# Row softmax on one core: stores moved from the load queue to a queue of their own, with a ring of three large slots

## The chip, the cores and the metric

The kernel runs on one core of a Trainium2 chip. The metric is device time in microseconds (us), the median of several executions. Ratios between kernels are the mean time of one kernel's fast runs over the mean time of the other's fast runs of the same rounds, so they are not quite the ratio of the medians quoted beside them.

## The reference

```python
def setup_inputs():
    batch, seq, dim = 32, 512, 1024
    return {"x": np.random.randn(batch, seq, dim).astype(np.float32), "temperature": 0.5}

def reference(x, temperature):
    scaled = x / temperature
    shifted = scaled - np.max(scaled, axis=-1, keepdims=True)
    exp_x = np.exp(shifted)
    return (exp_x / np.sum(exp_x, axis=-1, keepdims=True)).astype(np.float32)
```

There are 16,384 rows of 1,024 floats: 67.1 MB are read and 67.1 MB written. With 128 partitions each partition handles 128 rows of 4 KiB.

## The kernel before

All data passes through one ring in SBUF, 48 rows per partition. The kernel loads 8 rows per partition at a time (4 MiB, one contiguous piece of 32 KiB per partition), so the ring has six slots. VectorE takes the maximum of a group of four rows, ScalarE computes the exponentials and their sums in place, VectorE divides in place, and the slot is stored.

```python
LOADS = [8] * 16
STORES = [[8]] * 16
RING = 48
GROUP = 4
AHEAD = 2
# ... (cut)
    with tc.tile_critical():
        for kind, i, after in _queue(LOADS, STORES, places, AHEAD):
            if kind == "load":
                for b in range(after + 1):          # stores that free this slot
                    if b > done_to:
                        nc.sync.wait_ge(stored[b], 16)
                # ... nc.sync.dma_start(ring <- x).then_inc(loaded[i], 16)
            else:
                nc.sync.wait_ge(scaled, part_end[i])
                # ... nc.sync.dma_start(out <- ring).then_inc(stored[i], 16)
        # ...
        for g in range(len(groups)):
            exponential(g)                          # ScalarE's whole program

        for g in range(len(groups) + 1):            # VectorE's program
            if g < len(groups):
                maximum(g); shift(g)                # maximum waits for loaded[i]
            if g > 0:
                invert(g - 1); divide(g - 1)        # divide raises scaled
```

`_queue` puts loads and stores into one fixed order for SP's queue. `AHEAD = 2` means that two more stores are issued before SP waits for the store that frees a slot for the next load.

## Time and profile before

| | before |
|---|---|
| time, median of the first 3 runs | 321.85 us (321.15 to 322.12) |
| span of the profiled run | 319.9 us |
| VectorE (DVE) busy | 235.4 us, 74% |
| ScalarE (ACT) busy | 149.6 us, 47% |
| the one data queue busy | 97.9% of the span of 16 DMA engines |
| moved | 134.22 MB, mean 420 GB/s |

From the page of before, the span in 40 slices (tenths of the 16 DMA engines' time, then GB/s) and the queue table:

```profile
DMA  8999999999999999999999999999999999999992
GB/s 328 406 447 443 410 459 406 386 448 438 418 451 406 447 422 430 443 418 434 434 426 443 426 430 431 430 447 422 430 419 434 438 426 434 434 426 443 430 430 115
...
q1 hardware_dynamic: 4608, 134.22, 97.9%
```

The DMA engines are full in every slice but the first and the last. Single slices scatter because a transfer's bytes count in the slice where a packet is recorded; the mean of the 38 slices between is 430.

The costliest groups of the same page (line, engine, operation, busy us and mean ns, then idle time before it and who ended it):

```profile
L131 ACT ACTIVATE ring<-ring,bias 128x1024 f32<-128x1024 f32 x128 | 145.4, 1137 | 145.9 <-DVE bias L123 145.9
L113 DVE TENSOR_REDUCE top<-ring 128x4 f32<-128x4096 f32 x32 | 141.3, 4416 | 59.7 <-DMA ring<-in_x_dram 59.7
L150 DVE TENSOR_SCALAR ring<-ring,recip 128x1024 f32<-128x1024 f32 x128 | 87.7, 749 | 1.1
```

Both compute engines have slack. VectorE waits 59.7 us for loads; it isn't the bottleneck.

The DMA issues on SP's queue up to 92 us, without the first six loads, from the timeline of before (start us, duration us; the first line merges three issues, and its duration runs from the first to the last of them):

```profile
32.87 29.88 SPq L171 DMA_DIRECT2D out_dram<-ring  x3
72.68 0.34 SPq L165 DMA_DIRECT2D ring<-in_x_dram  x1
77.19 0.33 SPq L171 DMA_DIRECT2D out_dram<-ring  x1
82.36 0.34 SPq L165 DMA_DIRECT2D ring<-in_x_dram  x1
91.97 0.33 SPq L171 DMA_DIRECT2D out_dram<-ring  x1
92.35 0.43 SPq L165 DMA_DIRECT2D ring<-in_x_dram  x1
```

The load at 72.68 waited for the first store. The second and third stores had been issued before it (the x3 of the first line), so the DMA engines had work while the load was being released.

**A bookkeeping for the DMA engines.** The trace holds a record for each packet of data. The records don't name the engine; a packet that starts where another ends, within a few ns, is taken as its successor on the same engine. Undisturbed, a 32 KiB packet takes 1.213 us and the next one on its engine starts 4 ns before it ends, so one engine needs 1.209 us per 32 KiB and 16 engines move 433.6 GB/s. 134.22 MB at that rate are 309.5 us. For any run I split the time until the last transfer's completion arrives, 0.3 to 0.4 us after the last packet ends, into three parts: *work* (309.5 us, always the same), *idle* (engines with no packet, as a mean over the 16) and *slow* (the remainder: packets that took longer than usual). For before, the last completion arrives at 318.4 us: 309.5 work + 6.2 idle + 2.7 slow. The last 1.5 us of the span follow it. Of the 6.2 us idle, 2.2 are the start; most of the rest is the end, where the engines finish 4.8 us apart.

### The profile page before, as it was taken

The page shows a single profiled execution, that of the slowest core. Times are in us where ns is not written, and L with a number is a line of the kernel's source. Part 1 is how long each engine was busy: PE and PEld are TensorE (multiplying, and loading weights), DVE is VectorE, ACT ScalarE, POOL GpSimd, SP SyncE. Part 2 cuts the span into 40 slices and gives each one's busy share as a digit, 9 for nine tenths or more (in the row PEclk, how much of TensorE's full clock was granted, in tenths as well). Part 3 has the DMA queues.
Part 4 walks back from the last instruction along what each step waited for, and adds up shares of the span by engine and source line. Part 5 has one row for each costly group of instructions (what it writes and reads, how often), then busy time and mean ns, then how long its engine had stood idle before and what let it go on. Part 6 is the DMA issues. An engine that isn't in the chain of part 4 may idle for free.

```text
span 319.9 us, 568 instructions
## 1 busy us (share of the span) xinstructions
DVE 235.4 (74%) x224; ACT 149.6 (47%) x257; POOL 0.2 (0%) x4
## 2 busy tenths in 40 slices
DVE  0399999999996966939679495794948949498300
ACT  1076666665555551635516355163553625546000
POOL 0000000000000000000000000000000000000000
DMA  8999999999999999999999999999999999999992
GB/s 328 406 447 443 410 459 406 386 448 438 418 451 406 447 422 430 443 418 434 434 426 443 426 430 431 430 447 422 430 419 434 438 426 434 434 426 443 430 430 115
DMA packets 4612, 134.25 MB, mean 420 GB/s; under 512 B 512, under 2 KB 512, under 8 KB 512
## 3 DMA queue, kind: packets, MB, share of 16 engines
q1 hardware_dynamic: 4608, 134.22, 97.9%
q14 instruction: 4, 0.03, 0.0%
HBM read 67.11 MB, written 67.11 MB: 420 GB/s over the span
## 4 chain that ended last, share of the span: by engine, by line
DMA 60%; DVE 30%; ACT 3%; issue 0%; SPq 0%
DMA ring<-in_x_dram 35%; DMA out_dram<-ring 26%; DVE top L113 18%; DVE ring L150 11%; ACT ring L131 3%; DVE bias L123 1%; DVE recip L144 0%; SPq L219 0%; SPq L156 0%
## 5 line engine op out<-in xcount | busy, mean ns | idle before, releaser
L131 ACT ACTIVATE ring<-ring,bias 128x1024 f32<-128x1024 f32 x128 | 145.4, 1137 | 145.9 <-DVE bias L123 145.9
L113 DVE TENSOR_REDUCE top<-ring 128x4 f32<-128x4096 f32 x32 | 141.3, 4416 | 59.7 <-DMA ring<-in_x_dram 59.7
L150 DVE TENSOR_SCALAR ring<-ring,recip 128x1024 f32<-128x1024 f32 x128 | 87.7, 749 | 1.1
L131 ACT ACTIVATION_READ_ACCUMULATOR ring<-ring,bias 128x1 f32 x128 | 23.9, 187 | 0.0
L144 DVE RECIPROCAL recip<-sums 128x4 f32<-128x4 f32 x32 | 5.5, 171 | 2.0 <-ACT ring L131 2.0
L123 DVE TENSOR_SCALAR bias<-top 128x4 f32<-128x4 f32 x32 | 5.4, 170 | 1.1
L131 ACT ACT_TABLE_LOAD x1 | 1.3, 1283 | 0.9 <-SPq L156 0.9
L205 POOL MEMSET const-bfloat16-1.0<- 128x1 bf16 x1 | 0.1, 101 | 0.0
L205 POOL MEMSET const-uint8-127<- 128x1 uint8 x1 | 0.1, 101 | 0.0
L205 POOL MEMSET const-float32-0.0<- 128x1 f32 x1 | 0.1, 98 | 0.2 <-issue 0.2
L205 POOL MEMSET const-float32-1.0<- 128x1 f32 x1 | 0.1, 98 | 0.0
## 6 DMA issues: line engine op xcount, KB each, us to landing
ring<-in_x_dram SPq DMA_DIRECT2D x16, 4096.0 KB, 49.0
out_dram<-ring SPq DMA_DIRECT2D x16, 4096.0 KB, 40.5
```

The costliest lines, as they stand in the source:

```text
L113: nc.vector.tensor_reduce(out=top[:, r : r + k], in_=ring[:, s : s + k, :], axis=mybir.AxisListType.X, op=extreme,).then_inc(topped, 1)
L123: nc.vector.tensor_scalar_mul(bias[:, r : r + k], in0=top[:, r : r + k], scalar1=-scale).then_inc(biased, 1)
L131: ins = nc.scalar.activation(ring[:, s + a, :], ring[:, s + a, :], mybir.ActivationFunctionType.Exp, bias=bias[:, r + a : r + a + 1], scal ...
L144: nc.vector.reciprocal(recip[:, r : r + k], sums[:, r : r + k]).then_inc(inverted, 1)
L150: ins = nc.vector.tensor_scalar_mul(ring[:, s + a, :], in0=ring[:, s + a, :], scalar1=recip[:, r + a : r + a + 1])
L205: nc = _bacc.Bacc("TRN2", target_bir_lowering=False, num_devices=1)
```

## The change

Loads stay on SP's queue; stores go on ScalarE's. Neither queue has an order relative to the other: a load waits only for the stores that covered its slot, a store only for its division. The ring becomes three slots of 16 rows, so a transfer is 8 MiB in pieces of 64 KiB. The last 32 rows are handled in smaller parts. The intent is larger pieces and no fixed order that could hold back a ready transfer.

```diff
-LOADS = [8] * 16
-STORES = [[8]] * 16
+LOADS = [16] * 7 + [8] * 2
+STORES = [[16]] * 6 + [[8, 8]] + [[8]] * 2
 RING = 48
 GROUP = 4
-AHEAD = 2
 # ... (_queue and the loop over it removed)
+    def load(i):
+        # ... waits on nc.sync for stored[] of the parts that cover this slot
+        nc.sync.dma_start(out=ring[:, s : s + k, :], in_=dram(xf, r, k, i)).then_inc(
+            loaded[i], 16
+        )
+    def store(n):
+        l, s, r, k = parts[n]
+        nc.scalar.wait_ge(scaled, part_end[n])
+        nc.scalar.dma_start(out=dram(of, r, k, l), in_=ring[:, s : s + k, :]).then_inc(
+            stored[n], 16
+        )
 # ...
-        for g in range(len(groups)):
-            exponential(g)
+        for i in range(len(LOADS)):
+            load(i)
+        # ... SP waits for the stores that are left
+        for g in range(len(groups) + 1):
+            if g < len(groups):
+                exponential(g)
+            for n in range(len(parts)):
+                if part_end[n] == g:
+                    store(n)
```

VectorE's program is unchanged. On VectorE, a slot's last group is divided only after the maximum of the next slot's first group, which waits for the next load. In ScalarE's program, the store stands behind the exponentials of that same group.

More of the change, by code (lines that the diff above doesn't have):

```diff
@@ L28, in _places @@
     return places
-def _queue(loads, stores, places, ahead):
-    flat = [(i, n) for i, ks in enumerate(stores) for n in range(len(ks))]
-    last = {i: n for n, (i, _) in enumerate(flat)}
-    order, given = [], 0
-    for i, k in enumerate(loads):
-        over = [
-            b
-            for b in range(i)
-            if places[b] < places[i] + k and places[i] < places[b] + loads[b]
-        ]
-        after = max((last[b] for b in over), default=-1)
-        while given <= after + ahead and after >= 0 and flat[given][0] < i:
-            order.append(("store", given, None))
-            given += 1
-        order.append(("load", i, after))
-    order += [("store", n, None) for n in range(given, len(flat))]
-    return order
 @with_exitstack
@@ L153, in divide @@
         ins.then_inc(scaled, 1)
-    done_to = -1
-    with tc.tile_critical():
-        for kind, i, after in _queue(LOADS, STORES, places, AHEAD):
-            if kind == "load":
-                for b in range(after + 1):
-                    if b > done_to:
-                        nc.sync.wait_ge(stored[b], 16)
-                done_to = max(done_to, after)
-                s, r, k = places[i], first[i], LOADS[i]
-                nc.sync.dma_start(
-                    out=ring[:, s : s + k, :], in_=dram(xf, r, k, i)
-                ).then_inc(loaded[i], 16)
-            else:
-                l, s, r, k = parts[i]
-                nc.sync.wait_ge(scaled, part_end[i])
-                nc.sync.dma_start(
-                    out=dram(of, r, k, l), in_=ring[:, s : s + k, :]
-                ).then_inc(stored[i], 16)
-        for b in range(len(parts)):
-            if b > done_to:
-                nc.sync.wait_ge(stored[b], 16)
-        for g in range(len(groups)):
-            exponential(g)
+    def load(i):
+        nonlocal free_to
+        s, r, k = places[i], first[i], LOADS[i]
+        for n, (l, s1, r1, k1) in enumerate(parts):
+            if l < i and s1 < s + k and s < s1 + k1 and n > free_to:
+                for b in range(free_to + 1, n + 1):
+                    nc.sync.wait_ge(stored[b], 16)
+                free_to = n
+        nc.sync.dma_start(out=ring[:, s : s + k, :], in_=dram(xf, r, k, i)).then_inc(
[7 more added lines that the diff above has]
+        )
+    free_to = -1
+    with tc.tile_critical():
+        for i in range(len(LOADS)):
+            load(i)
+        for b in range(free_to + 1, len(parts)):
+            nc.sync.wait_ge(stored[b], 16)
+        for g in range(len(groups) + 1):
[4 more added lines that the diff above has]
+                    store(n)
         for g in range(len(groups) + 1):
```

## The prediction

> **What bounds the kernel now.** The DMA engines. The page's slices show DMA at 9 tenths or more in 38 of 40 slices, 420 GB/s over the span of 319.9 us; the queue table has one queue busy for 97.9%. VectorE is busy 235.4 us (74%), ScalarE 149.6 us (47%): both have slack. The usual packet time in the trace is 1.213 us for 32 KiB, 432 GB/s on 16 engines; 134.22 MB at that rate is 310.6 us. The other 9 us are the start (first slice 328 GB/s: about 2.4 us without data), some slow packets, and the engines drifting apart (a transfer's 16 completions lie 0.5 us apart at the start, 4.7 us at the end). There is no DMA gap in the middle: when a store releases a load, two more stores already stand in the queue. So at most 3% can be won.
>
> **What the change does.** VectorE's and ScalarE's work keeps its order; ScalarE also issues ten stores (0.33 us each on SP). The ring has three slots of 16 rows instead of six of 8. The Trainium skill, "DMA: Bandwidth & Descriptors", section "Issuing engines are not separate DMA queues", says DMAs of all issuers run on the same 16 engines and interleave; the trace of before has one queue, so it shows nothing of this. I take it that sharing is even and adds no bandwidth. Larger packets give about 1 us at most (estimate: cost per packet above that page's 435 GB/s ceiling).
>
> **The critical path: hand-overs.** I walked the new schedule with the trace's durations: 19.4 us per 16-row transfer (16 x 1.21), 7.4 us per group of four on VectorE (4.42 + 2.74 + 0.2), 4.65 us on ScalarE. Three first loads fill the DMA until 60 us; store 0 is issued at about 59 us, just in time. From there each load needs the whole store before it in its slot. Store n can start only about 9 us after load n+1 landed (the divide of a slot's last group stands behind the maximum of the next slot's first group, the issue behind that group's exponentials). So load n+2 starts before store n and lands first; store n ends alone, and nothing is queued until its completion releases the next load. Each hand-over leaves all engines idle for completion, issue and first packet: about 1.4 us from issue to data, as at the start of before, plus waiting for the slowest engine, 2.4 us together. There are five (loads 3 to 7): +12 us. Against it, the drift is reset (-3 us), packets give -1 us; mixing costs perhaps +2 us (at load-to-store turns in before, packets took 0.1 to 0.5 us longer). The tail stays DMA-bound. Sum: 319.9 + 12 - 4 + 2 = 330 us of span, about 331 us of time.
>
> **Prediction:** 331 us, range 321 to 341. Faster by over 2%: 0.05; within 2%: 0.30; slower by over 2%: 0.65.
>
> **What would show it.** Two DMA queues of 67 MB each; dips in the DMA slices at about 80, 121, 162, 204 and 245 us; the chain that ended last made of alternating loads and stores, 19 us alone and up to 39 us shared; VectorE waiting for loads longer than the present 59.7 us; packets in mixed stretches lasting twice as long, total GB/s there 425 to 432.
>
> **What would make it wrong.** If the engines favour one queue, a load may still run when a store ends, and hand-overs vanish: about 318 us. If mixed reading and writing is faster than one queue, faster still. If mixing is slow (5%), 340 us or more.

## The result, and the profile after

The changed kernel takes 337.58 us (336.35 to 338.23, 4 runs) against 321.99 us (321.15 to 322.59) for before; the ratio is 1.0482 with a 95% interval of 1.0443 to 1.052. It is slower.

From its page, the slices, the queue table and the costliest groups:

```profile
DMA  9898989888898987989599988989889999999995
GB/s 375 375 500 375 492 382 492 376 383 343 297 484 375 500 351 273 492 382 492 258 375 414 461 382 367 375 376 500 375 375 340 391 449 418 418 429 429 433 433 258
...
q1 hardware_dynamic: 1296, 67.11, 49.4%
q10 hardware_dynamic: 1440, 67.11, 46.2%
...
L109 ACT ACTIVATE ring<-ring,bias 128x1024 f32<-128x1024 f32 x128 | 145.5, 1138 | 165.0 <-DVE bias L101 165.0
L91 DVE TENSOR_REDUCE top<-ring 128x4 f32<-128x4096 f32 x32 | 141.3, 4415 | 79.4 <-DMA ring<-in_x_dram 79.4
L128 DVE TENSOR_SCALAR ring<-ring,recip 128x1024 f32<-128x1024 f32 x128 | 87.7, 749 | 1.1
```

There are now two queues of 67.11 MB. Compute is unchanged to within a nanosecond (4415 ns, 749 ns, 1138 ns), so the 16.0 us of extra span are not computing. VectorE's wait for loads grew from 59.7 to 79.4 us.

Ten-microsecond stretches of after that hold the moments when a store ends (columns: stretch, length, busy time of VectorE, ScalarE and GpSimd, clock, DMA share, GB/s):

```profile
80.00:90.00 10.00, 9.93 (x8) 6.10 (x12) 0.00 (x0) 1.00 0.90 315
120.00:130.00 10.00, 9.93 (x8) 4.64 (x8) 0.00 (x0) 1.00 0.88 315
160.00:170.00 10.00, 5.63 (x5) 1.04 (x1) 0.00 (x0) 1.00 0.79 315
200.00:210.00 10.00, 4.98 (x4) 0.40 (x1) 0.00 (x0) 1.00 0.73 315
250.00:260.00 10.00, 9.93 (x8) 4.64 (x8) 0.00 (x0) 1.00 0.69 265
```

The same first two stretches of before, for comparison:

```profile
80.00:90.00 10.00, 9.86 (x12) 5.52 (x9) 0.00 (x0) 1.00 1.01 436
120.00:130.00 10.00, 7.62 (x8) 3.03 (x5) 0.00 (x0) 1.00 1.00 433
```

Five times the rate falls from about 433 to 315 GB/s or less. The chain of work that ended last shows what ties these moments together (start us, duration us, what):

```profile
57.51 24.74 DMA out_dram<-ring
82.25 0.02 issue
82.27 37.45 DMA ring<-in_x_dram
119.72 0.02 issue
119.74 4.43 DVE top L91
124.17 0.02 issue
124.19 0.18 DVE bias L101
124.37 0.02 issue
124.40 2.85 ACT ring L109 x5
127.25 40.05 DMA out_dram<-ring
167.30 0.02 issue
167.31 37.61 DMA ring<-in_x_dram
```

A store ends at 82.25 and releases a load at 82.27. That load lands at 119.72; VectorE takes one maximum and then divides the last group of the older slot, and only then, at 127.25, is the next store of the chain issued. The chain names ScalarE at this step, but the timeline of after shows that the store was issued 0.03 us after the division ended (124.48 + 2.74 = 127.22), with the third of the group's four exponentials still running:

```profile
124.48 2.74 DVE L128 TENSOR_SCALAR ring<-ring,recip 128x1024 f32<-128x1024 f32 x4
126.68 1.14 ACT L109 ACTIVATE ring<-ring,bias 128x1024 f32<-128x1024 f32 x1
127.25 0.34 ACTq L149 DMA_DIRECT2D out_dram<-ring  x1
127.81 1.13 ACT L109 ACTIVATE ring<-ring,bias 128x1024 f32<-128x1024 f32 x1
```

The store ends at 167.30 and releases another load. At 82.25 nothing else was queued: by the packet records the last packet of the old store ends at 81.79, its completion releases the load at 82.25, the load's first packet starts at 83.24, and the last engine's first packet at 84.14. All engines are idle for 1.45 us. A finer look at the windows of after confirms it: no packet starts from 81 to 83 us.

```profile
81.00:83.00 2.00, 2.00 (x1) 0.46 (x2) 0.00 (x0) 1.00 0.00 0
83.00:85.00 2.00, 1.93 (x5) 0.79 (x1) 0.00 (x0) 1.00 1.47 524
```

(In such short windows a packet counts where it starts, so a share can also exceed 1.)

The bookkeeping of after: the last completion arrives at 334.5 us = 309.5 work + 14.1 idle + 10.8 slow (rounded). Against before that is 7.9 us more idle and 8.1 us more slow, together the 16.0 us. Per cycle from one hand-over to the next it is 1.9 to 2.3 us idle (1.3 to 1.45 us of it on all engines at once) and 1.7 to 2.0 us slow, against 38.7 us of work. The slow packets sit in two places: the first load packet after the gap (3.0 us on average for the 64 KiB pieces, instead of 2.418 us), and the load packets just ahead of the first packet of the store that joins (up to 4.0 us). Once both queues run, packets take 2.418 us: of the 164 packets that start between 135 and 161 us, every one takes 2.418 us and every one follows a packet of the other queue.

### The profile page after: what moved, and what is told of

The parts are those of the page before. It is cut to its first block, busy times and chain, and to the rows that moved or that the text cites. A ratio compares the mean times of both kernels' runs of the same rounds, so it can differ in the third digit from the quotient of the medians.

```text
span 335.9 us, 554 instructions
## 1 busy us (share of the span) xinstructions
DVE 234.9 (70%) x224; ACT 149.6 (45%) x257; POOL 0.2 (0%) x4
## 3 DMA queue, kind: packets, MB, share of 16 engines
q1 hardware_dynamic: 1296, 67.11, 49.4%
q10 hardware_dynamic: 1440, 67.11, 46.2%
HBM read 67.11 MB, written 67.11 MB: 400 GB/s over the span
## 4 chain that ended last, share of the span: by engine, by line
DMA 74%; DVE 15%; ACT 5%; issue 0%; SPq 0%
DMA ring<-in_x_dram 43%; DMA out_dram<-ring 31%; DVE top L91 10%; ACT ring L109 5%; DVE ring L128 4%; DVE bias L101 0%; DVE recip L122 0%; SPq L142 0%; SPq L206 0%; SPq L154 0%
## 5 line engine op out<-in xcount | busy, mean ns | idle before, releaser
L109 ACT ACTIVATE ring<-ring,bias 128x1024 f32<-128x1024 f32 x128 | 145.5, 1138 | 165.0 <-DVE bias L101 165.0
L91 DVE TENSOR_REDUCE top<-ring 128x4 f32<-128x4096 f32 x32 | 141.3, 4415 | 79.4 <-DMA ring<-in_x_dram 79.4
```

The costliest lines, as they stand in the source:

```text
L91: nc.vector.tensor_reduce(out=top[:, r : r + k], in_=ring[:, s : s + k, :], axis=mybir.AxisListType.X, op=extreme,).then_inc(topped, 1)
L109: ins = nc.scalar.activation(ring[:, s + a, :], ring[:, s + a, :], mybir.ActivationFunctionType.Exp, bias=bias[:, r + a : r + a + 1], scal ...
```

## The experiments

Theory H: with three slots, each of five loads is released by a store behind which nothing is queued, and that hand-over costs the idle and the slow time. Rival M: two queues mix loads and stores on each engine, and the mixing costs. Rival P: 64 KiB pieces are slow. Two more readings blamed one of the two orders that tie a store to the next load.

The bookkeeping of all runs, in us (last completion = 309.5 work + idle + slow, to about 0.1 us; one profiled execution of each kernel):

| run | queues, slot rows | time, median | ratio to before, 95% interval | idle | slow |
|---|---|---|---|---|---|
| before | 1, 8 | 321.85 | | 6.2 | 2.7 |
| after | 2, 16 | 337.58 | 1.0482 (1.0443 to 1.052) | 14.1 | 10.8 |
| two_queues_8 | 2, 8 | 318.80 | 0.9912 (0.9893 to 0.9931) | 4.1 | 1.9 |
| pieces_32k | 2, 16 | 335.48 | 1.0428 (1.0404 to 1.0452) | 14.0 | 9.0 |
| early_store | 2, 16 | 326.21 | 1.0137 (1.0103 to 1.017) | 7.8 | 4.2 |
| one_queue_8_ahead0 | 1, 8 | 356.22 | 1.1068 (1.1034 to 1.1103) | 23.6 | 20.0 |
| divide_early | 2, 16 | 331.12 | 1.0308 (1.0237 to 1.038) | 8.3 | 10.2 |
| store_first | 2, 16 | 338.36 | 1.0496 (1.0461 to 1.0531) | 15.3 | 10.6 |
| two_queues_12 | 2, 12 | 320.54 | 0.9958 (0.9898 to 1.0018) | 5.6 | 2.1 |
| one_queue_16_ahead0 | 1, 16 | 336.68 | 1.0453 (1.0422 to 1.0484) | 13.4 | 10.5 |

All eight experiments gave correct results. The first four ran on one chip against one set of runs of before (median 321.77 us), the last four likewise (322.33 us).

### two_queues_8

```diff
-LOADS = [16] * 7 + [8] * 2
-STORES = [[16]] * 6 + [[8, 8]] + [[8]] * 2
+LOADS = [8] * 16
+STORES = [[8]] * 16
```

> The changed kernel with the slots of before: loads of 8 rows in six slots (32 KiB pieces), loads on SP's queue, stores on ScalarE's. Theory H (hand-overs: with three slots nothing is queued when a store completes; each of five costs about 2.7 us of idle engines plus a first slow packet, and about 1 us when the store joins the load): with six slots other loads or stores are always queued, so 319 to 325 us, no dip below 9 tenths in the middle slices. Rival M (two queues mix loads and stores on each engine, and that costs): stays at 335 us or more, because the mixing is as long or longer. Rival P (64 KiB pieces are slow): also 319 to 325, so this run tells M from H and P, not H from P.

Measured: 318.80 us. Its slices:

```profile
DMA  8999999999999999999999999999999999999995
GB/s 327 405 455 409 389 447 430 438 432 430 438 426 438 426 442 418 447 434 426 438 430 442 422 438 426 435 430 434 442 426 439 426 442 422 438 426 438 438 422 227
```

No dip is left, although the two queues mix loads and stores from 60 us on: until 300 us about four packets in five follow one of the other queue. M falls, and with it my +2 us for mixing: between 60 and 300 us the slow time here is 0.3 us in all. This version even beats before by 0.9%, with an interval clear of 1: the engines finish 1.9 us apart instead of 4.8 us, which is 2.1 of the 2.9 us by which the last completion comes earlier. Whether the second queue or the freed order does this was not tested apart.

### pieces_32k

```diff
-        block = block.rearrange("(p k) d -> p k d", p=P, k=LOADS[i])
-        return block[:, r - first[i] : r - first[i] + k, :]
+        block = block.rearrange("(h p k) d -> p h k d", p=P, k=8)
+        a = (r - first[i]) // 8
+        return block[:, a : a + k // 8, :, :]
```

The ring's side of each transfer is viewed as `p (h k) d` in the same way.

> The changed kernel with the same slots, transfers and order, but each 16-row transfer moves two pieces of 32 KiB per partition instead of one of 64 KiB (the rows of a slot are dealt to partitions in two blocks of 8). H: 336 to 340 us, the five dips stay. P: falls to about 322 us. M: unchanged or a little slower, as the engines change between queues twice as often: at 0.1 us for each change it would be 343 us or more.

Measured: 335.48 us, half a microsecond under the range that I gave for H, and nowhere near P's 322. Idle time is as in after (14.0 against 14.1), slow time 1.8 us less. So piece size isn't the cause. At most it makes the slow packets of a hand-over a little longer.

### early_store

```diff
 # ScalarE
+            for n in range(len(parts)):
+                if part_end[n] == g:
+                    store(n)
             if g < len(groups):
                 exponential(g)
-            for n in range(len(parts)):
-                if part_end[n] == g:
-                    store(n)
 # VectorE
+            early = 0 < g < len(groups) and groups[g][0] != groups[g - 1][0]
+            if early:
+                invert(g - 1)
+                divide(g - 1)
             if g < len(groups):
                 maximum(g)
                 shift(g)
-            if g > 0:
+            if g > 0 and not early:
                 invert(g - 1)
                 divide(g - 1)
```

> The changed kernel with two orders changed: VectorE divides the last group of a slot before it takes the maximum of the next slot, and ScalarE issues the store before the next slot's exponentials. Slots, queues, sizes as in the change. H: the second store of a cycle no longer waits for the next load, so at most of the hand-overs another transfer is running or queued: 323 to 329 us, one or two dips (near 82 us) left instead of five. M and P: 335 to 340 us, as the bytes mixed and the pieces are the same or the mixed time is longer.

Measured: 326.21 us. The issues of the third store and the loads around it, from the timeline of early_store:

```profile
118.33 0.34 ACTq L149 DMA_DIRECT2D out_dram<-ring  x1
124.56 36.55 SPq L142 DMA_DIRECT2D ring<-in_x_dram  x2
151.62 0.34 ACTq L149 DMA_DIRECT2D out_dram<-ring  x1
```

In after the same store was issued at 127.25 us, 2.7 us behind the load that its predecessor had released. Here it is issued at 118.33 us, while its predecessor still runs, so the load at 124.56 us finds the engines busy. The bookkeeping from 100 to 220 us shows less than 0.1 us of idle and slow time together in 120 us; the first hand-over, near 82 us, is still there. It has the same two queues, slots, sizes and bytes as the change, and 11 us of the 16 are gone. What remains are that one hand-over and 2.9 us idle at the end.

### one_queue_8_ahead0

```diff
-AHEAD = 2
+AHEAD = 0
```

> The kernel before with AHEAD = 0 instead of 2: one queue, 32 KiB pieces, six slots, but SP issues no further store before it waits for the one that frees a slot. H: each of the ten loads after the sixth is a hand-over with an empty queue: ten times about 2.7 us, 345 to 352 us. M and P: same as before, 322 us, as there is neither a second queue nor a larger piece.

Measured: 356.22 us, more than I expected. Its slices:

```profile
DMA  8999999979898798898996979989979898999996
GB/s 322 447 414 436 451 414 411 415 299 355 355 403 370 303 399 359 355 388 318 359 455 270 393 303 414 366 333 363 414 299 359 351 414 355 444 444 414 444 444 296
```

Before's own queue, slots and pieces, with the stores ahead taken away, get ten hand-overs and lose 34.7 us of span (354.6 against 319.9), about 3.5 us each: 1.7 us idle and 1.7 us slow when the totals are compared with those of before ((23.6 - 6.2) / 10 and (20.0 - 2.7) / 10). (The first of these hides about 3 us that the engines' smaller spread at the end gave back: idle time after 300 us is 0.2 us here and 3.5 us in before.) So a hand-over costs this much with one queue and 32 KiB pieces too. My expected 2.7 us left out most of the slow part.

### divide_early

Only VectorE's half of early_store.

```diff
+            early = 0 < g < len(groups) and groups[g][0] != groups[g - 1][0]
+            if early:
+                invert(g - 1)
+                divide(g - 1)
```

> Only one half of early_store: VectorE divides a slot's last group before the next slot's maximum, but ScalarE still issues the store behind the next slot's first exponentials, which wait for the next load. H: the store is still tied to the next load, the five hand-overs stay: 335 to 340 us. If VectorE's order alone caused the late store, 323 to 329 us.

Measured: 331.12 us, below my 335 to 340: a miss. The second transfers of a cycle now lie a little differently. From its timeline:

```profile
122.72 1.15 ACT L109 ACTIVATE ring<-ring,bias 128x1024 f32<-128x1024 f32 x1 [7.55 <-DVE bias L101]
122.75 0.34 ACTq L149 DMA_DIRECT2D out_dram<-ring  x1
```

The third store is issued 0.03 us after the next slot's first exponential starts. So ScalarE's order ties the store to the next load and its maximum, but not to the time of the exponentials; it no longer waits for the division, which my expectation did not consider. It is issued at 122.75 us, 1.4 us before the second one's completion arrives at 124.17 us, and its first packets start 0.2 us before the second one's last packet ends. From the second hand-over on the engines are never all idle at once; idle time falls to 8.3 us. The slow time stays at 10.2 us. So the slow part doesn't need an idle gap; a store that comes just before the old one ends is too late to avoid it, while one that comes 6 us earlier, as in early_store, avoids it.

### store_first

Only ScalarE's half of early_store.

```diff
+            for n in range(len(parts)):
+                if part_end[n] == g:
+                    store(n)
             if g < len(groups):
                 exponential(g)
-            for n in range(len(parts)):
-                if part_end[n] == g:
-                    store(n)
```

> The other half: ScalarE issues the store before the next slot's exponentials, but VectorE still divides a slot's last group behind the next slot's maximum, which waits for the next load. H: the store is still tied to the next load, only about 1.9 us earlier; five hand-overs stay: 334 to 340 us. If the place of the store in ScalarE's program alone were the cause, 323 to 329 us.

Measured: 338.36 us, no gain. VectorE's division still stands behind the next load. ScalarE's order alone is not the cause; VectorE's alone gives a part; both together give 11 us.

### two_queues_12

```diff
-LOADS = [16] * 7 + [8] * 2
-STORES = [[16]] * 6 + [[8, 8]] + [[8]] * 2
+LOADS = [12] * 10 + [8]
+STORES = [[12]] * 9 + [[8, 4]] + [[8]]
```

> The changed kernel with four slots of 12 rows (48 KiB pieces; ten loads of 12 and one of 8, the last stores in smaller parts). H: with a fourth slot a load is released while the next store is under way or queued, so no hand-over with empty queues: 317 to 323 us. If slow time grew with the size of a piece or transfer, it would lie between the 318.8 us of 8 rows and the 337.6 us of 16, about 328 us.

Measured: 320.54 us (318.76 to 323.37), equal to before within the noise. With a fourth slot the hand-overs are gone (idle 5.6, slow 2.1), and the time is not near the 328 us of a gradual effect of size. This run alone changes slots and sizes together; early_store kept both and recovered most of the time, so it is the hand-overs that count.

### one_queue_16_ahead0

```diff
 # in the kernel before
-LOADS = [8] * 16
-STORES = [[8]] * 16
-AHEAD = 2
+LOADS = [16] * 7 + [8] * 2
+STORES = [[16]] * 6 + [[8, 8]] + [[8]] * 2
+AHEAD = 0
```

> The kernel before (one queue, SP issues everything) with the loads and stores of the change (three slots of 16 rows, 64 KiB pieces) and AHEAD = 0, as with three slots nothing can be issued further ahead without waiting for itself. H: five hand-overs with an empty queue as in the change, so about the same time, 333 to 339 us. M (the second queue is to blame): near 322 us.

Measured: 336.68 us, with idle 13.4 and slow 10.5 as in after. With the slots of the change and one queue the loss is all there. So the second queue isn't needed for it.

## Why the prediction was right

The predicted time was 331 us with a range of 321 to 341 and the larger chance on slower; the measured 337.58 us lies inside, towards its upper end. The mechanism of the hand-overs was right. But of the 16.0 us of extra span the sum had only 10: slow packets brought 8.1 us where it had +2 for mixing and -1 for larger pieces. The upper end of the range had been argued from slow mixing, which did not happen. That the number still fell inside is partly luck.

- **DMA-bound before: right.** Work at full rate is 309.5 us of the 319.9 us span, and compute did not change.
- **Five hand-overs: right.** Dips were predicted near 80, 121, 162, 204 and 245 us; the stores that free a slot end at 82.3, 124.5, 167.3, 209.8 and 252.3 us. In four of the five the load of the cycle lands before the store; the first has only the store. early_store, two_queues_12 and one_queue_8_ahead0 take hand-overs away or add them, and the time follows.
- **Why a store comes late: right in the main.** The store waits for the next load, its maximum and the division behind it; untying both orders recovered 11 us. The time of the exponentials wasn't part of the wait: the store came 7.5 us after the load landed (119.72 to 127.25 us) instead of the 9 us predicted.
- **Cost of the idle part: slightly too high.** I said 2.4 us each, +12 us; it was about 2.0 us each, 10 us. The gap from issue to first data, put at 1.4 us, was 1.0 us (82.27 to 83.24 us); with the 0.5 us from the last packet's end to the release (81.79 to 82.25 us) all engines stood idle for 1.45 us. The drift gave back about 2 us (the idle time at the end fell from 3.5 to 1.2 us) instead of 3.
- **"mixing costs perhaps +2 us": the term that was mis-sized.** Slow packets cost 8.1 us more than before, and mixing isn't what they come from: once both queues run, packets take their normal 2.418 us. Each hand-over pays a slow first packet after the gap and a slow load packet ahead of the first store, about 1.7 us together. Before pays these once: about 0.65 us at the start and 0.95 us between 40 and 80 us, where the first store begins. Six starts at that cost instead of one would account for nearly all of it (6 x 1.6 = 9.6 of 10.8 us).
- **Larger pieces, -1 us: not borne out, small.** Undisturbed packets did gain: the next one starts 2.414 us after a 64 KiB packet against 2 x 1.209 us for two of 32 KiB, about 0.4 us in all. But the slow packets of the hand-overs grew with the piece: pieces_32k had 1.8 us less slow time and was, if anything, faster.
- **"Packets in mixed stretches lasting twice as long": wrong.** Here the engines took whole packets of the two queues in turn (164 of 164), so a packet isn't stretched; a transfer takes longer because its packets wait.

What stays open is the mechanism of the slow packets. They appear at hand-overs in one queue and in two, and in divide_early even without an idle gap. No run here shows what the engine does in them.

## What to carry to other kernels

When DMA is the bottleneck, ask of each transfer that frees a buffer what else is queued at the moment it completes; if the answer is nothing, each such moment cost 3 to 4 us here, whatever queue it was on. Prefer more, smaller slots over fewer, larger ones once the packets are at full rate (32 KiB was), and look for in-order programs that tie a ready store to the next load. Two queues with six slots, without any fixed order, were the best version here (318.80 us, 0.9% under before).

## What the Trainium skill lacked or had wrong

- "DMA: Bandwidth & Descriptors", section "Issuing engines are not separate DMA queues": it says that transfers from several issuers interleave on the same engines and that only sequencer time is saved. The first half agrees (164 of 164 followed packets alternated between the queues, at no loss). It lacks that two queues without a fixed order can come out a little ahead: 0.9% in two_queues_8, where the engines ended 1.9 us apart instead of 4.8 us. Queue and order were not tested apart.
- The same page, section "Queues, rings and completion order", says that an engine drains a whole packet, typically of about 9 to 17 descriptors, before it changes rows. It gives no size in bytes. Here the engines changed after each recorded packet of 64 KiB, one piece of one partition; the trace doesn't show how many descriptors such a packet has, so the figure of 9 to 17 is neither confirmed nor refuted.
- The same page, "Where 436 GB/s comes from": 435 GB/s as the ceiling agrees with the 433.6 GB/s of undisturbed packets. The limit of about 358 GB/s that the same passage gives for transfers between HBM and SBUF did not bind here, with one core running.
- No page has the slow packets of such a hand-over: 3.0 us for the first load packets and up to 4.0 us for those ahead of the joining store, instead of 2.418 us; about 1.7 us per hand-over.
